# A two-layer encoder on one core: the products that add back to the residual stream, in seven products over pairs of pages

## The chip, the cores and the metric

The kernel runs on one core of one Trainium2 chip. The time is device microseconds (us) of one launch. Engines: PE (TensorE, matmuls), DVE (VectorE), ACT (ScalarE), POOL (GpSimd), SP (SyncE, which here only issues DMAs). Each engine works through its own queue in order; semaphores order the engines among each other. SBUF is the on-chip memory, PSUM the eight accumulator banks of PE, DRAM the memory behind the DMAs.

## The reference

1024 tokens, width 1024, two layers, all in float32:

```python
for layer in range(DEPTH):
    if layer % 2 == 0:                       # layer 0
        y = even_mixer(...)                  # attention (8 heads) and 2-D Fourier mixing, concatenated (1536 wide), @ w_out
    else:                                    # layer 1
        z = gelu(x @ w_in); u, v = split(z)  # 2048 wide each
        v = layer_norm(v); s = spatial mixing of v in chunks of 128 tokens + b_s
        y = (u * s) @ w_out                  # o_out in the kernel
    x = layer_norm(DN_ALPHA * x + y)
    x = layer_norm(DN_ALPHA * x + (silu(x @ w_gate) * (x @ w_up)) @ w_down)   # 2816 wide between
```

Four products go back to the 1024-wide stream: w_out (1536 to 1024), down of layer 0 (2816 to 1024), o_out (2048 to 1024), down of layer 1. They are what the change is about, and each ends with the residual and a layer norm.

## The kernel before

A product in float32 is made of three matmuls in a reduced format: each operand is split into a high part (a cast by ACT, L131) and a low part (the rest, a subtraction by DVE, L132), and `mm3` (L137 to L139) issues high x high, high x low, low x high. A matmul has a 128x128 stationary operand and up to 512 moving columns. Every operand that comes from DRAM or from another engine passes through such a split.

The hidden activations lie in DRAM as *pages*: a page is 128 hidden columns by all 1024 tokens, the hidden columns on the partitions. w_out reads 12 pages (`mix`), down 22 (`ha`, `hb`), o_out 16 (`tp`). A page's weight is 128 rows by 1024 columns.

`reduce` is the plain product over these pages. `load` brings in a pair of pages (two weights of 128x1024, and 512 tokens of both pages) and splits the three tiles; `mm` adds four tiles of 128 tokens by two halves of 512 columns to the eight PSUM banks, and this is done for each half of the tokens (`blk`). `residual` loads four tiles of the stream; POOL multiplies them by the gain of the last norm and adds its bias (L387, L388), for tokens 0 to 3 and 4 to 7 apart. `tail` adds the accumulators, makes the norm's statistics (L398, L399), normalises (L407) and stores the tile. `turn` calls `operands`: PE transposes the tile (L309), ACT scales it on the way out (L311), and DVE and ACT make the seven left operands of the next product from it.

What reads the stream (gate/up, u, v) goes *in seven products*, after Strassen and Winograd: a 2x2 block product made with seven block products in place of eight, and with sums of blocks. `operands` and `right_operands` make these sums, `seven` runs the products of one unit (A11, A12, S1, S2, A22, S4, S3 by `b11`, `b21`, `t1`, `t2`, `t4`, `b22`, `t3`), `kept` copies a bank to SBUF (L512), `emit` adds them up. Unit 0 of `ffn` runs in two halves of 256 columns, so that the first half of the tokens can start before the second is turned. `v_pair` does the same for v. In `spatial`, POOL multiplies u by the mixed v (L706) and stores the page (L709).

Order: instructions are issued in the order written and then moved by a scheduler that works with priorities, so each engine's queue is a mixture of neighbouring steps. PE runs w_out from 555 to 692 us, gate/up of layer 0 to 1126, down 0 to 1374, v to 1537, u and spatial mixing to 1728, o_out to 1935, gate/up of layer 1 to 2354, down 1 to 2600. Attention and Fourier mixing come before 555.

Of the kernel before, what the change touches and what calls it, by code (L numbers as in the profile page):

```python
# [9 lines left out]
F32 = mybir.dt.float32  # L10
# [102 lines left out]
class Trunk:  # L113
# [104 lines left out]
    def page_pair(self, p0, p1, blk):  # L218
        r = self.raw_tile()
        for i, p in enumerate((p0, p1)):  # L220
            self.nc.sync.dma_start(r[:, i * 512:(i + 1) * 512], p[:, blk * 512:(blk + 1) * 512])
        hi, lo = self.wpair()
        self.split(hi, lo, r)
        return hi, lo


    def run(self):
        tc, nc, a = self.tc, self.nc, self.a
        with ExitStack() as top:
# [14 lines left out]
            pages = [D_("ha", [P, S], 22), D_("tp", [P, S], 16), D_("hb", [P, S], 22)]  # L244
# [5 lines left out]
            with ExitStack() as ms:  # L250
# [5 lines left out]
                self.xo = tuple(xp.tile([P, 7, 2, 4, 256], F32R, name=f"xo{x}") for x in "hl")  # L256
                self.mp = ms.enter_context(self.pool("main", "right"))
                order = [8, 9, 10, 11, 0, 1, 2, 3, 4, 5, 6, 7]
                x_in = [a["x"][t * P:(t + 1) * P, :] for t in range(NT)]
                down = lambda l: [a["w_down"][l, j] for j in range(22)]  # L260
# [5 lines left out]
                pend = self.reduce([a["w_out"][k] for k in order], [mix[k] for k in order], x_in, None, (0, 0), xs[0], self.ahead, lambda: pre(0))  # L266
                self.ffn(w0[0], gate_up(0), pages[0], pend)
                vw = []
                pend = self.reduce(down(0), pages[0], xs[0], (0, 0), (0, 1), xs[1], None, lambda: vw.append(self.v_first()))
                left = self.spatial(vw[0], pages[1], pend)  # L270
                pend = self.reduce([a["o_out"][j] for j in range(16)], pages[1], xs[1], (0, 1), (1, 0), xs[2], None, lambda: pre(1), left)
                self.ffn(w0[1], gate_up(1), pages[2], pend)
                self.reduce(down(1), pages[2], xs[2], (1, 0), (1, 1), None)
# [8 lines left out]
    A11, A12, A22, S1, S2, S3, S4 = range(7)  # L282

# [3 lines left out]
    def turn_bank(self):  # L287

        i = (4, 5, 6, 7, 0, 1)[self.turns % 6]
        self.turns += 1  # L290
        self.stamp[i] = self.turns
        return self.bank(i)

    def m_tile(self, tag, bufs, shape):
        return self.mp.tile(list(shape), F32, tag=tag, name=self.name(tag), bufs=bufs)

    def x_tile(self):
        return self.m_tile("x", 4, (P, 1024))

    def operands(self, z, t, banks, gT, bT, A):  # L300

        nc = self.nc
        half, b, c = (t % 4) // 2, t // 4, slice(t % 2 * P, (t % 2 + 1) * P)
        xh, xl = self.xo
        op = lambda o: (xh[:, o, b, :, c], xl[:, o, b, :, c])
        w = self.m_tile("A", 2, (P, 8, P)) if half == 0 else self.x_tile().rearrange("p (k c) -> p k c", k=8)
        pss = [self.bank(i, (P, 4, P)) for i in banks]
        for k in range(8):
            nc.tensor.transpose(pss[k // 4][:, k % 4, :], z[:, k * P:(k + 1) * P], self.ident)  # L309
        for k in range(8):  # L310
            nc.scalar.activation(w[:, k, :], pss[k // 4][:, k % 4, :], AF.Identity, bias=bT[:, k:k + 1], scale=gT[:, k:k + 1])  # L311
# [8 lines left out]
        nc.vector.tensor_tensor(s, lo, hi, op=ALU.add)  # L320
        self.split(*op(self.S1), s)
        self.sub(s, s, a[:, 0:4, :])
        self.split(*op(self.S2), s)
        self.split(*op(self.A22), hi)
        self.sub(a[:, 4:8, :], a[:, 4:8, :], s)
        self.split(*op(self.S4), a[:, 4:8, :])
        self.sub(lo, a[:, 0:4, :], lo)
        self.split(*op(self.S3), lo)


    def reduce(self, ws, ps, resid, rgb, ln, keep, ahead=None, pre=None, left=()):

        left = list(left)
        nc, a = self.nc, self.a
        n = len(ws) // 2
        acc, A, xt, ops, z = {}, {}, {}, {}, {}
        xh, xl = self.xo
        flat = lambda o: tuple(x[:, o, 1].rearrange("p k c -> p (k c)") for x in (xh, xl))  # L340
        own = lambda: tuple(self.wx.tile([P, 1024], F32R, tag=t, name=self.name(t), bufs=1) for t in ("whi", "wlo"))
        sets = (lambda: [self.wpair() for _ in range(3)], lambda: [flat(o) for o in (2, 3, 4)], lambda: [flat(5), flat(6), own()])
        order = [0, 1, 2] * (n // 3) + [1, 2] if n % 3 == 2 else [0, 1, 2] * (n // 3 - 1) + [0, 1, 2]
        assert len(order) == n
        if keep is not None:
            gT, bT = (self.m_tile(x, 2, (P, 8)) for x in ("gT", "bT"))
            nc.gpsimd.dma_start(gT, a["ln_gT"][ln[0], ln[1]])
            nc.gpsimd.dma_start(bT, a["ln_bT"][ln[0], ln[1]])
        else:
            fg, fb = (self.bcast(self.m_tile("A", 2, (P, D)), a["ln_" + x][ln[0], ln[1]]) for x in "gb")  # L350
        self.less_weights()
        gb = self.pool("gb", "right")
        gp = gb.__enter__()
        if rgb is not None:
            rg, rb = (self.bcast(gp.tile([P, D], F32, name=self.name("r" + x)), a["ln_" + x][rgb[0], rgb[1]]) for x in "gb")

        def load(idx, blk):

            if (idx, blk) == (0, 0) and ahead is not None:
                ops[idx, blk] = ahead  # L360
                return
            pairs = sets[order[idx]]()
            u = []
            for i in range(2):
                r = self.raw(ws[2 * idx + i])
                self.split(*pairs[i], r)
                u.append(pairs[i])
            r = self.raw_tile()
            for i in range(2):
                self.nc.sync.dma_start(r[:, i * 512:(i + 1) * 512], ps[2 * idx + i][:, blk * 512:(blk + 1) * 512])  # L370
            self.split(*pairs[2], r)
            ops[idx, blk] = u, pairs[2]

        def mm(t, c, idx, i):
            us, (hh, hl) = ops[idx, t // 4]
            uh, ul = us[i]
            s, cc = slice(i * 512 + t % 4 * P, i * 512 + (t % 4 + 1) * P), slice(c * 512, (c + 1) * 512)
            if (t, c) not in acc:
                acc[t, c] = self.bank((0, 2, 4, 6, 2, 4, 6, 0)[t] + c)
            self.mm3(acc[t, c], (hh[:, s], hl[:, s]), (uh[:, cc], ul[:, cc]), idx == 0 and i == 0, idx == n - 1 and i == 1)  # L380

        def residual(ts):
            for t in ts:
                x = xt[t] = self.x_tile()
                nc.gpsimd.dma_start(x, resid[t])
# [4 lines left out]
        def tail(t, between=None):  # L390

            x, st = xt[t], self.small.tile([P, 2, 6], F32, tag="st", name=self.name("st"))
            for c in range(2):
                cc = slice(c * 512, (c + 1) * 512)
                for idx in (n - 2, n - 1):
                    for i in range(2):
                        mm(t, c, idx, i)
# [823 lines left out]
```

## Time and profile before

| | |
|---|---|
| median of 3 runs | 2611.92 us (2611.84 to 2617.37) |
| the profiled execution: its own time, its span | 2606.84 us, 2605.0 us |
| busy: PE, DVE, ACT, POOL | 2562.8, 1609.7, 1039.0, 362.4 us |
| granted PE clock, mean | 0.996 of full |
| moved by DMA | 293.5 MB, 113 GB/s on average |

The profile is one execution as the hardware profiler recorded it. A row of instructions has the line in the kernel, the engine, the operation, out<-in with the program's names (buffer numbers left out), the shape and count, then busy time in us and the mean of one in ns; behind the second bar stands how long the engine had idled ahead of these, and what ended it. A row of the timeline has the start in us, the time in us, and in brackets the idle time before. Matmuls are pipelined: one lasts longer than the distance to the next.

### The profile page before, as it was taken

How to read it: one execution, taken by the hardware profiler on the slowest of the kernel's cores; microseconds unless marked ns; L12 is line 12 of the kernel's file. 1: busy time of each engine (PE TensorE's matmuls, PEld its weight loads, DVE VectorE, ACT ScalarE, POOL GpSimd, SP SyncE). 2: the span in 40 equal slices, each digit the busy share in tenths (PEclk: the TensorE clock that was granted, in tenths of full speed). 3: DMA queues.
4: the chain of work that ended last, by engine and by line, in shares of the span. 5: the costliest groups of instructions: out<-in, count | busy, mean ns of one | idle time of the engine just before them, and what ended most of it. 6: DMA issues, size and time to landing. Idle time of an engine off the chain costs nothing.

```text
span 2605.0 us, 32916 instructions
## 1 busy us (share of the span) xinstructions
PE 2562.8 (98%) x12894; PEld 2156.7 (83%) x12894; DVE 1609.7 (62%) x2195; ACT 1039.0 (40%) x1609; POOL 362.4 (14%) x357
## 2 busy tenths in 40 slices
PE   9999999999999999999999999999999999999998
PEld 7878888888888888878789998878788888888877
DVE  4457677657765555564848667765785555546564
ACT  4335455545533333332526443333453333333221
POOL 1000000001000000030401025561400000003130
PEclk9999999999999999999999999999999999999999
DMA  5121111045222222255533244464532222235461
GB/s 174 39 84 44 33 39 43 21 148 187 96 93 86 73 89 75 93 192 167 182 125 122 85 128 140 138 207 160 175 117 89 81 82 81 81 119 186 148 213 70
DMA packets 98532, 293.51 MB, mean 113 GB/s; under 512 B 12712, under 2 KB 17480, under 8 KB 98376
## 3 DMA queue, kind: packets, MB, share of 16 engines
q1 hardware_dynamic: 75496, 213.23, 25.7%
q0 software_dynamic: 22880, 78.18, 8.1%
q8 instruction: 101, 1.65, 0.3%
q14 instruction: 55, 0.45, 0.1%
HBM read 223.72 MB, written 62.91 MB: 110 GB/s over the span
## 4 chain that ended last, share of the span: by engine, by line
PE 88%; DVE 5%; issue 3%; DMA 2%; POOL 1%; ACT 1%; SPq 0%; DVEq 0%; POOLq 0%; ACTq 0%
PE b L139 20%; PE b L137 20%; PE b L138 20%; PE b L751 6%; PE S L1137 6%; PE mm L137 4%; PE mm L138 4%; PE mm L139 4%; PE mm L1156 2%; DVE wlo L132 1%; DMA raw<-w_down 1%; DVE xol L132 1%; PE b L703 1%; PE b L309 1%; DVE st L399 0%
## 5 line engine op out<-in xcount | busy, mean ns | idle before, releaser
L139 PE MATMUL b<-xoh,wlo 128*128 128x512 f32 (+1 forms) x1928 | 746.5, 387 | 4.6 <-DVE wlo L132 4.6
L137 PE MATMUL b<-xoh,whi 128*128 128x512 f32 (+1 forms) x1928 | 747.7, 388 | 0.0
L138 PE MATMUL b<-xol,whi 128*128 128x512 f32 (+1 forms) x1928 | 745.2, 386 | 0.0
L132 DVE TENSOR_TENSOR wlo<-raw,whi 128x1024 fp32r<-128x1024 f32 (+2 forms) x353 | 445.9, 1268 | 462.0 <-ACT whi L131 437.0
L131 ACT CAST whi<-raw 128x1024 fp32r<-128x1024 f32 (+2 forms) x353 | 343.6, 976 | 716.9 <-PE b L138 480.1
L139 PEld LDWEIGHTS b<-xoh,wlo 128*128 128x128 f32 x1928 | 363.2, 188 | 83.2 <-DVE wlo L132 7.0
L137 PEld LDWEIGHTS b<-xoh,whi 128*128 128x128 f32 x1928 | 363.5, 189 | 76.6 <-DVE x L578 1.2
L138 PEld LDWEIGHTS b<-xol,whi 128*128 128x128 f32 x1928 | 363.2, 188 | 76.2 <-issue 0.2
L132 DVE TENSOR_TENSOR xol<-raw,xoh 128x1024 fp32r<-128x1024 f32 x130 | 167.1, 1305 | 174.5 <-ACT xoh L131 174.2
L131 ACT CAST xoh<-raw 128x1024 fp32r<-128x1024 f32 x130 | 133.6, 1053 | 258.8 <-PE b L139 123.1
L512 ACT COPY ct<-b 128x512 f32<-128x512 f32 (+1 forms) x240 | 136.9, 570 | 171.7 <-PE b L139 136.0
L139 PE MATMUL b<-xoh,xol 128*128 128x512 f32 x416 | 163.0, 392 | 3.3 <-DVE rs L201 3.3
L137 PE MATMUL b<-xoh 128*128 128x512 f32 x416 | 164.2, 395 | 0.0
L138 PE MATMUL b<-xol,xoh 128*128 128x512 f32 x416 | 162.4, 390 | 0.0
L127 DVE TENSOR_TENSOR raw<-raw,raw 128x512 f32<-128x512 f32 (+1 forms) x176 | 133.1, 756 | 24.8 <-DMA raw<-o_v 12.9
L137 PE MATMUL b<-whi,whi 128*128 128x512 f32 x320 | 127.3, 398 | 7.5 <-ACT whi L131 6.0
L139 PE MATMUL b<-whi,wlo 128*128 128x512 f32 x320 | 126.6, 396 | 4.0 <-DVE wlo L132 4.0
L751 PE MATMUL b<-whi,xoh 128*128 128x256 f32 x448 | 126.3, 282 | 0.0
L751 PE MATMUL b<-whi,xol 128*128 128x256 f32 x448 | 126.3, 282 | 0.0
L751 PE MATMUL b<-wlo,xoh 128*128 128x256 f32 x448 | 126.2, 282 | 0.0
L138 PE MATMUL b<-wlo,whi 128*128 128x512 f32 x320 | 126.1, 394 | 0.0
L573 DVE TENSOR_TENSOR ct<-b,ct 128x512 f32<-128x512 f32 (+1 forms) x92 | 61.3, 666 | 103.3 <-PE b L139 103.2
(278 smaller groups left out, 4023.3 us busy)
## 6 DMA issues: line engine op xcount, KB each, us to landing
raw<-w_down SPq DMA_DIRECT2D x88, 512.0 KB, 3.8
raw<-w_gate SPq DMA_DIRECT2D x44, 512.0 KB, 3.7
raw<-w_up SPq DMA_DIRECT2D x44, 512.0 KB, 3.6
raw<-o_out SPq DMA_DIRECT2D x32, 512.0 KB, 5.0
raw<-w_out SPq DMA_DIRECT2D x24, 512.0 KB, 5.7
xs<-x POOLq DMA_DIRECT2D x24, 512.0 KB, 2.9
x<-xs POOLq DMA_DIRECT2D x24, 512.0 KB, 4.6
ha<-x POOLq DMA_DIRECT2D x22, 512.0 KB, 2.9
```

Source lines behind the costliest of these rows:

```text
L127: self.nc.vector.tensor_tensor(out, a, b, op=ALU.subtract)
L131: self.nc.scalar.copy(hi, src)
L132: (eng or self.nc.vector).tensor_tensor(lo, src, hi.bitcast(F32), op=ALU.subtract)
L137: mm(ps, lh, rh, start=start, stop=False, skip_group_check=skip)
L138: mm(ps, lh, rl, start=False, stop=False, skip_group_check=skip)
L139: mm(ps, ll, rh, start=False, stop=stop, skip_group_check=skip)
L309: nc.tensor.transpose(pss[k // 4][:, k % 4, :], z[:, k * P:(k + 1) * P], self.ident)
L512: self.nc.scalar.copy(t, ps)
L573: nc.vector.tensor_tensor(sb, ps, sb, op=op)
L751: nc.tensor.matmul(ps[:, i * 256:(i + 1) * 256], l[:, o, b, k, c], r[:, k, :], start=start and k == 0 and i == 0 and m == 0, stop=k == 3 a ...
L1137: nc.tensor.matmul(sc[:, kb, :], l[:, s], r[:, kb * 512:(kb + 1) * 512], start=i == 0, stop=i == 4)
L1156: nc.tensor.transpose(ps[:, k, :], p[:, kt * P:(kt + 1) * P], self.ident)
```

## The change

All four `reduce` products now go in seven as well. Two pages form the 2x2 blocks with two halves of tokens: for pages h0, h1 (each cut into 512 tokens `lo` and 512 `hi`) and weights w0, w1 (each cut into two halves of the columns) there are seven products, each summed over all pairs of pages (in groups `g` of two pairs, the first of one if their number is odd) before the next one begins, in the order p = 1, 5, 6, 4, 7, 2, 3. A product has four slots of 128 tokens by 512 columns, so four PSUM banks. Sums of pages (SA, SB) and of weights (TA, TB) that the products need are made ahead by POOL (`combine`: two loads, four additions or subtractions of 128x512, two stores) and kept in DRAM; during attention for w_out, during gate/up for down, during v and u for o_out. The last pair's page sum is made while p = 1 runs.

```diff
+    def combine(self, tile, srcs, dsts, pages):
+        nc, lo, hi = self.nc, self.LO, self.HI
+        tt = nc.gpsimd.tensor_tensor
+        r0, r1 = tile(), tile()
+        for r, s in zip((r0, r1), srcs):
+            nc.gpsimd.dma_start(r, s)
+        if pages:
+            tt(r1[:, hi], r0[:, hi], r1[:, hi], op=ALU.add)
+            tt(r0[:, hi], r0[:, lo], r0[:, hi], op=ALU.subtract)
...
+        for r, d in zip((r0, r1), dsts):
+            nc.gpsimd.dma_start(d, r)
+    def source(self, st, p, m):
...
+        return {1: (h0[:, lo], w0[:, lo]), 2: (h1[:, lo], w1[:, lo]), 3: (sb[:, lo], w1[:, hi]), 4: (h1[:, hi], tb[:, lo]),
+                5: (sb[:, hi], ta[:, lo]), 6: (sa[:, lo], tb[:, hi]), 7: (sa[:, hi], ta[:, hi])}[p]
+    def stream(self, st, p, ms, raws, pairs):
...
+        for side in range(2):
+            r, (h, l) = raws(), pairs()
+            for i, m in enumerate(ms):
+                self.nc.sync.dma_start(r[:, i * 512:(i + 1) * 512], self.source(st, p, m)[side])
+            self.split(h[:, :n], l[:, :n], r[:, :n])
     def reduce(...):
-        sets = (lambda: [self.wpair() for _ in range(3)], lambda: [flat(o) for o in (2, 3, 4)], lambda: [flat(5), flat(6), own()])
...
+        for p in (1, 5, 6, 4, 7, 2):
+            for g in range(n):
+                load(p, g)
+                if p == 1 and g == 0:
...
+                    residual(0)
+                if p == 1 and g == 1:
+                    residual(1)
+                if p == 2:
+                    spread([lambda s=s: normed1(s) for s in slots], g, n)
+                for s in slots:
+                    mm(p, g, s)
...
+                if p == 1 and g == n - 1:
+                    self.page_job(st, M - 1)
+        for g in range(n):
+            load(3, g)
+            if g < n - 2:
+                for s in slots:
+                    mm(3, g, s)
+                spread([lambda s=s: turn1(s) for s in slots], g, n - 2)
...
+        return [lambda s=s: turn0(s) for s in slots], lambda: [sums(s) for s in slots]
     def ffn(...):
-            u0, u1 = unit(0, w0, 0), unit(0, w0, 1)
-            self.go(u0, 2)
-            pend[0]()
...
+        def store(j):
+            nc.gpsimd.dma_start(st["H"][j], page.pop(j))
+            if j % 2 == 0:
+                self.weight_job(st, j // 2, tile)
+            elif j >= 3:
+                self.page_job(st, j // 2 - 1, tile)
+        u0 = unit(0, w0, "yq")
+        turns[0]()
+        self.go(u0, 1)
+        turns[1]()
+        turns[2]()
+        self.go(u0, 1)
+        turns[3]()
```

Beside this, a unit of gate/up goes through its products in the order t4, t1, b11, b21, t2, b22, t3 with all 512 columns, unit 0 too; v goes in the order 4, 5, 1, 2, 6, 3, 7; the tiles of the second half of the tokens are turned during p = 3 (`turn1`), those of the first half (`turn0`) and the sums of both after it, inside the next stage. The tiles `x`, `y`, `q` take the place of `ct`, `A`, `S`.

What moves in the queues, at the two places that matter below. First POOL at the start of down 0; `x` are stream tiles, `xs` their copies in DRAM, `rg`, `rb` the gain and bias of the norm, `ha` the pages. Before:

```order
L583 DMA ha_134<-x_9304 128x1024
L385 DMA x_9585<-xs_3_92 128x1024
L387 TENSOR_TENSOR x_9573<-x_9573,rg_9418 128x1024
L387 TENSOR_TENSOR x_9577<-x_9577,rg_9418 128x1024
L388 TENSOR_TENSOR x_9573<-x_9573,rb_9420 128x1024
L388 TENSOR_TENSOR x_9577<-x_9577,rb_9420 128x1024
```

The same place after, from the store of the last page (`h_21`) on; `gb` are the gain and bias, `x_9712`, `x_9713` and `raw` the tiles of the sums:

```order
L636 DMA h_21_206<-x_9692 128x1024
L304 TENSOR_TENSOR x_9713<-x_9712,x_9713 128x512
L420 TENSOR_TENSOR x_9734<-x_9734,gb_9746 128x1024
L305 TENSOR_TENSOR x_9712<-x_9712 128x512
L421 TENSOR_TENSOR x_9734<-x_9734,gb_9748 128x1024
L306 TENSOR_TENSOR x_9712<-x_9713,x_9712 128x512
L420 TENSOR_TENSOR q_9736<-q_9736,gb_9746 128x1024
L307 TENSOR_TENSOR x_9713<-x_9713,x_9712 128x512
L314 DMA ffn0SA_216<-x_9712 128x1024
```

It ends, 14 multiplies and adds after the last page's store, with the sum of the last pair:

```order
L420 TENSOR_TENSOR x_9733<-x_9733,gb_9746 128x1024
L421 TENSOR_TENSOR x_9733<-x_9733,gb_9748 128x1024
L304 TENSOR_TENSOR raw_9965<-raw_9964,raw_9965 128x512
L305 TENSOR_TENSOR raw_9964<-raw_9964 128x512
L306 TENSOR_TENSOR raw_9965<-raw_9965,raw_9964 128x512
```

Before, four tiles went through POOL here and nothing of the product waited for them; now all eight do, and page sums stand between and behind them.

Second ACT where w_out ends and gate/up 0 begins; L311 (after: L337) is the scaling of a transposed tile, L131 the cast of an operand, L512 (L579) the copy of a bank. Before:

```order
L512 COPY ct_6488<-b_6475 128x256
L311 ACTIVATE x_6490<-b_6491,bT_5313,gT_5312 128x128 x4
L311 ACTIVATE x_6490<-b_6492,bT_5313,gT_5312 128x128
L131 CAST xoh<-S_6431 128x4x128
L311 ACTIVATE x_6490<-b_6492,bT_5313,gT_5312 128x128
```

After:

```order
L337 ACTIVATE x_6571<-b_6572,bT_5575,gT_5574 128x128 x4
L337 ACTIVATE x_6571<-b_6573,bT_5575,gT_5574 128x128 x4
L131 CAST xah_6569<-x_6571 128x4x128 x2
L337 ACTIVATE x_6609<-b_6610,bT_5575,gT_5574 128x128 x4
L337 ACTIVATE x_6609<-b_6611,bT_5575,gT_5574 128x128 x4
L131 CAST xah_6569<-x_6609 128x4x128 x2
L337 ACTIVATE q_6632<-b_6633,bT_5575,gT_5574 128x128 x4
L337 ACTIVATE q_6632<-b_6634,bT_5575,gT_5574 128x128 x2
L579 COPY y_6607<-b_6594 128x512
```

Before, one tile's scaling stands here among the copies of unit 0; after, the tiles of the first half are scaled here one behind the other, into `xah`, which the third product of unit 0 reads whole.

More of the change, by code (lines that the diff above doesn't have):

```diff
@@ L265, in pre @@
                     w0[l] = self.right_operands(*gate_up(l)(0))
[L266 to L271, printed above, removed]
@@ L272, in run, with pre_v @@
[L272 to L273 removed]
+                def pre_v():
+                    w0["v"] = self.v_begin(0)
+                G = self.stage
+                pend = self.reduce(G["mix"], x_in, None, (0, 0), xs[0], self.ahead, lambda: pre(0))
+                self.ffn(w0[0], gate_up(0), G["ffn0"], pend)
+                pend = self.reduce(G["ffn0"], xs[0], (0, 0), (0, 1), xs[1], None, pre_v)
@@ L302, in operands, with turned @@
+    def turned(self, z, banks, tile, gT, bT):
         nc = self.nc
[L303 to L306, printed above, removed]
+        w = tile.rearrange("p (k c) -> p k c", k=8)
         pss = [self.bank(i, (P, 4, P)) for i in banks]
@@ L323, in operands @@
[L323 to L331, printed above, removed]
-        left = list(left)
[L336 to L341, printed above, removed]
-        sets = (lambda: [self.wpair() for _ in range(3)], lambda: [flat(o) for o in (2, 3, 4)], lambda: [flat(5), flat(6), own()])
-        order = [0, 1, 2] * (n // 3) + [1, 2] if n % 3 == 2 else [0, 1, 2] * (n // 3 - 1) + [0, 1, 2]
-        assert len(order) == n
+        return w[:, 0:4, :], w[:, 4:8, :]
@@ new lines, in reduce, with pairs @@
+    def reduce(self, st, resid, rgb, ln, keep, ahead=None, pre=None, left=()):
+        nc, a = self.nc, self.a
+        lo, hi = self.LO, self.HI
+        left = list(left)
+        M = len(st["W"]) // 2
+        groups = [[0]] * (M % 2) + [[m, m + 1] for m in range(M % 2, M, 2)]
+        n = len(groups)
+        self.less_weights()
+        if self.xa is not None:
+            self.xpool.__exit__(None, None, None)
+        self.xpool = self.pool("rx", "left")
+        rx = self.xpool.__enter__()
+        cells = [tuple(x[:, b].rearrange("p k c -> p (k c)") for x in self.left(o)) for o in (4, 6, 5) for b in range(2)]
+        count = [0]
+        def pairs():
+            count[0] += 1
+            return cells[(count[0] - 1) % len(cells)]
+        raws = lambda: rx.tile([P, D], F32, tag="rx", name=self.name("rx"), bufs=6)
+        tmp = lambda: rx.tile([P, D], F32, tag="gb", name=self.name("gb"), bufs=2)
@@ L354, in reduce @@
[L354 to L360, printed above, removed]
-                return
[L362 to L385, printed above, removed]
+        token = lambda half, s: s // 2 * 4 + half * 2 + s % 2
@@ L386, in residual, with add @@
+        def add(half, s, c, p, first=False, op=ALU.add):
+            x = xt[half, s][:, c]
+            if first:
+                nc.vector.scalar_tensor_tensor(x, x, ALPHA, acc[p, s], ALU.mult, op)
+            else:
+                nc.vector.tensor_tensor(x, x, acc[p, s], op=op)
+        def residual(half):
+            for s in range(4):
+                x = xt[half, s]
+                nc.gpsimd.dma_start(x, resid[token(half, s)])
                 if rgb is not None:
@@ new lines, in ffn, with v_cells @@
+        turns[2]()
+        self.go(u0, 1)
+        turns[3]()
+        u1 = unit(1, self.right_operands(*weights(1)), "yq")
+        self.go(u1, 2)
+        sums()
+        self.go(u0, 5)
+        store(0)
+        self.go(u1, 5)
+        store(1)
+        for j in range(2, 22):
+            self.go(unit(j, self.right_operands(*weights(j))))
+            store(j)
+    def v_cells(self, pi):
+        a = self.a
+        b11, b12, b21, b22 = (self.raw(a["o_v"][pi * 4 + i]) for i in (0, 2, 1, 3))
+        w = {}
```

555 lines of the change are left out of this document (284 added, 271 removed).

## The prediction

> **What bounds the kernel now.** I read the page first (busy time by engine, then the chain that ended last), then busy time by stage.
>
> ```profile
> span 2605.0 us, 32916 instructions
> PE 2562.8 (98%) x12894; PEld 2156.7 (83%) x12894; DVE 1609.7 (62%) x2195; ACT 1039.0 (40%) x1609; POOL 362.4 (14%) x357
> PE 88%; DVE 5%; issue 3%; DMA 2%; POOL 1%; ACT 1%; SPq 0%; DVEq 0%; POOLq 0%; ACTq 0%
> ```
>
> TensorE is busy for 98% of the span and is 88% of the chain: matmuls taken off PE come off the time, unless PE then waits. The stages, cut where PE goes from one product to the next:
>
> ```profile
> 555.00:692.00 137.00, 137.00 (x633) 113.87 (x632) 90.25 (x120) 63.73 (x104) 15.35 (x26) 1.00 0.55 187
> 692.00:1126.00 434.00, 434.00 (x1964) 356.87 (x1964) 248.55 (x337) 174.53 (x259) 15.89 (x29) 1.00 0.27 91
> 1126.00:1374.00 248.00, 242.54 (x1083) 199.52 (x1082) 149.71 (x139) 86.35 (x124) 55.95 (x33) 0.99 0.47 156
> 1374.00:1537.00 163.00, 162.97 (x1366) 162.49 (x1365) 114.19 (x175) 80.46 (x125) 21.41 (x38) 1.00 0.34 115
> 1549.00:1728.00 179.00, 177.56 (x887) 148.66 (x885) 135.58 (x257) 66.31 (x95) 92.44 (x104) 1.00 0.47 149
> 1728.00:1935.00 207.00, 197.81 (x943) 164.44 (x942) 136.66 (x159) 84.12 (x141) 66.56 (x45) 0.98 0.48 159
> 1935.00:2354.00 419.00, 419.00 (x1841) 342.05 (x1840) 236.49 (x314) 160.99 (x228) 13.29 (x25) 1.00 0.29 95
> 2354.00:2600.00 246.00, 237.85 (x1037) 194.87 (x1035) 138.20 (x124) 57.66 (x57) 55.15 (x29) 0.99 0.45 151
> ```
>
> After the stretch come busy PE, weight loads, DVE, ACT, POOL, the granted clock, DMA share, GB/s. In order: w_out, gate/up 0, down 0, v, u with the spatial mixing, o_out, gate/up 1, down 1. The three reduces down 0, o_out and down 1 leave 5.46 + 9.19 + 8.15 = 22.8 us of PE idle; the rest nearly none. These three are also where POOL's multiplies and adds lie, and there DVE shows this (the first row is DVE's, the others POOL's):
>
> ```profile
> 1136.37 18.66 DVE L132 TENSOR_TENSOR wlo<-raw,whi 128x1024 fp32r<-128x1024 f32 x1 [5.29 <-ACT whi L131]
> 1135.02 4.80 POOL L387 TENSOR_TENSOR x<-x,rg 128x1024 f32<-128x1024 f32 x2
> ...
> 1149.19 4.75 POOL L388 TENSOR_TENSOR x<-x,rb 128x1024 f32<-128x1024 f32 x2
> ```
>
> Eight POOL operations of 4.76 / 2 = 2.38 us run back to back, and one DVE split is recorded for all of that time. The same place at other moments goes in turn:
>
> ```profile
> 1260.93 1.22 DVE L132 TENSOR_TENSOR wlo<-raw,whi 128x1024 fp32r<-128x1024 f32 x1
> 1262.06 2.90 DVE L320 TENSOR_TENSOR S<-x 128x512 f32<-128x512 f32 x1
> 1264.88 2.90 DVE L132 TENSOR_TENSOR xol<-x,xoh 128x512 fp32r<-128x512 f32 x1
> 1261.23 6.00 POOL L387 TENSOR_TENSOR x<-x,rg 128x1024 f32<-128x1024 f32 x2 [1.12 <-DMA x<-xs]
> ```
>
> The first split takes 1.22 us without POOL beside it; then each DVE operation waits out one POOL operation. So DVE with two inputs in SBUF and POOL tensor operations exclude each other: their times add.
>
> **The change, step by step.** Prices:
>
> ```profile
> 1084.70 0.39 PE L138 MATMUL b<-xol,whi 128*128 128x512 f32 x1
> ...
> 1088.19 0.39 PE L138 MATMUL b<-xol,whi 128*128 128x512 f32 x1
> L387 POOL TENSOR_TENSOR x<-x,rg 128x1024 f32<-128x1024 f32 x24 | 68.1, 2849 | 27.3 <-DMA x<-xs 27.3
> L706 POOL TENSOR_TENSOR x<-x,whi 128x512 f32<-128x512 f32 x16 | 22.4, 1399 | 24.4 <-DVE whi L704 16.2 <-PE b L138 7.4 <-issue 0.7
> L385 POOL DMA_DIRECT2D x<-xs x24 | 13.4, 558 | 46.2 <-issue 21.4 <-DMA xs<-x 10.7 <-DMA tp<-x 6.5
> L131 ACT CAST whi<-raw 128x1024 fp32r<-128x1024 f32 x291 | 304.9, 1051 | 597.5 <-PE b L138 385.6 <-PE mm L138 49.8 <-DMA raw<-w_down 46.2
> L132 DVE TENSOR_TENSOR wlo<-raw,whi 128x1024 fp32r<-128x1024 f32 x291 | 402.7, 1389 | 288.8 <-ACT whi L131 263.9 <-POOL x L706 12.0 <-PE mm L1156 6.2
> L127 DVE TENSOR_TENSOR raw<-raw,raw 128x512 f32<-128x512 f32 x156 | 108.9, 698 | 11.7 <-DMA raw<-o_u 6.5 <-DMA raw<-w_up 2.0 <-DVE wlo L704 0.8
> L694 DVE TENSOR_SCALAR wlo<-wlo,vmv,vrs 128x128 f32<-128x128 f32 x64 | 26.3, 492 | 3.9 <-DMA wlo<-vd 3.9
> L131 ACT CAST xoh<-A 128x512 fp32r<-128x512 f32 x36 | 21.6, 651 | 2.4 <-DVE A L127 2.4
> L311 ACT ACTIVATE x<-b,bT,gT 128x128 f32<-128x128 f32 x96 | 36.2, 478 | 5.4 <-PE b L309 5.4
> ha<-x POOLq DMA_DIRECT2D x22, 512.0 KB, 2.9
> raw<-ha SPq DMA_DIRECT2D x44, 256.0 KB, 3.9
> tp<-x POOLq DMA_DIRECT2D x16, 512.0 KB, 3.5
> raw<-tp SPq DMA_DIRECT2D x32, 256.0 KB, 4.3
> ```
>
> Fewer matmuls. Before, the reduces take 72 pages x 48 = 3456 matmuls of 512 columns; after, 36 pairs x 7 products x 4 slots x 3 = 3024. The two rows are the first and the last of 16 starts in a stretch without a wait: (1088.19 - 1084.70) / 15 = 0.233 us for a matmul. 432 x 0.233 = **-100 us**: 16.8 in w_out (6 pairs), 30.7 in each down (11 pairs), 22.3 in o_out (8). Unit 0 of the gate/up stages, now done whole, keeps its columns: 0.
>
> The waits that the three reduces have now lose their place: between 0 and -22.8; the last one's end stays, so **-20**.
>
> What is added on other engines: 72 sums on POOL, each 2 loads, 4 operations of 512 columns, 2 stores, all in POOL's one queue. On DVE the additions of product banks to the tiles grow in number; they read PSUM on one side, and they come at the ends of products, beside 12 matmuls each: 0 but for what is named below. On SP the loads become more and smaller (256 KB for 512), 0.52 MB per pair and product of 12 x 0.233 = 2.79 us, which is 188 GB/s; the w_out row shows 187 with PE never idle: 0.
>
> Start of down 0 and down 1. All eight residual tiles now go through POOL when the reduce starts, mixed with the last page sums, and every sum must be stored before the second product (p=5) ends. After the last page's store stand 14 residual operations, 8 of a sum and 8 DMA issues: 14 x 2.38 + 8 x 1.3 + 8 x 0.55 = 48 us; the last page is ready some 4 us after the reduce starts and landings on the way hold the queue some 5 (estimates, from the landing rows), the store 2.9, the load 3.9, cast and split 1.05 + 1.22: 66. PE needs it when p=1 and all but the last group of p=5 (9 of 11 pairs) are done: 30.7 + 9 x 2.79 = 56. So 10 us even if DVE costs POOL nothing. DVE has about 20 splits of 1.22 us in that time; one for one they add 24, but some come before the tile loads land: ends 10 and 31 a stage, taken **24 each, 48**. What is queued behind POOL there: nothing PE needs before.
>
> By the Trainium skill (SBUF — State Buffer, Who interferes with whom), the engine that issues first keeps the shared ports for its whole instruction, and the other fully blocks. The trace agrees at 1262 (2.9 us against 2.4 of POOL's one operation), not at 1136, where eight went by. With the page's rule alone a split waits for one POOL operation at most and each such stage would lose about 24; with starvation up to 31, by the rows above.
>
> Start of o_out: the last four spatial multiplies stand behind 14 residual operations: 14 x 2.38 + 9 x 1.3 + 7 us of issues and landings = 52 until the last page is stored, then its landing 3.5, the load for the sum 4, the sum 5.2, its landing 3.5, load and split 4.3 + 2.3: 75. PE gets to it after p=1 (22.3), three of the four groups of p=5 (16.8) and two groups of p=6, which stand ahead (11.2): 50. Ends 20 and 36 (with the splits), taken **30**.
>
> The two gate/up starts. Before, half of the tokens are turned before the reduce ends; now all four turns of the first half, for ACT 4 x (8 x 0.478 + 2 x 0.651) = 20.5 us, come after its last product, and A11 reads all four. PE has 24 matmuls (5.6 us) and 32 transposes of 128 columns (at least a quarter of a 512-column matmul, 1.9; taken as 3) to cover them: about 12 us of waiting. After such a wait PE runs slower for a while:
>
> ```profile
> 1282.42 0.50 PE L137 MATMUL b<-whi,whi 128*128 128x512 f32 x1 [2.71 <-ACT whi L131]
> ...
> 1284.70 0.63 PE L137 MATMUL b<-whi,whi 128*128 128x512 f32 x1
> ...
> 1287.69 0.53 PE L138 MATMUL b<-wlo,whi 128*128 128x512 f32 x1
> ```
>
> (Seven steps in 2.99 us, 0.43 each: about +2 with the first ones.) Ends 10 and 22, taken **15 each, 30**. The same at v, where A11 comes third, with weight sums on POOL beside it: ends 5 and 20, **13**. In w_out, the shortest reduce, POOL's last sums and the normalisation's DVE work lie in p=2 and p=3: ends 0 and 10, **5**.
>
> u with the mixing: per group PE has 177.56 / 8 = 22 us; POOL now has 8 operations x 1.3 = 10.4. DVE has 4 subtractions (L127, 2.8), splits of 3.5 tiles (4.3) and 16 normalisations of v (L694, 64 for each of two tiles over 8 groups, 0.49: 7.9): 15. Together 25, 3 over what PE has, 24 in 8 groups; but part of DVE's work reads PSUM or meets POOL waiting for a DMA. Ends 0 and 36 (store-to-load waits on POOL added), half of 24 taken: **12**. Sums beside gate/up and attention: in the 434 us of a gate/up stage, 39 for two units, DVE has 248.55 / 11 = 23 and POOL gets 8 x 1.3 = 10.4: 33 together fit, but not always at the right moment: ends 0 and 20, **6**.
>
> Sum: -100 - 20 + 48 + 30 + 30 + 13 + 5 + 12 + 6 = +24. The profiled execution took 2606.8 us (span 2605.0), so 2631; the median of the runs is 5 above it, so **2636**. All lower ends give -55, 2557; all upper ends +108, 2720.
>
> **Rivals.** (a) Faster: POOL's chain is not late, because the residual tiles' loads and the splits leave gaps that the sums fill, and waits come to half: -120 + 72 = -48, 2564. For it: waits of before hid mostly; the split of 18.66 us cost PE little:
>
> ```profile
> 1156.21 0.50 PE L139 MATMUL b<-whi,wlo 128*128 128x512 f32 x1 [1.61 <-DVE wlo L132]
> ```
>
> Against: there POOL had nothing that PE needed, now it has. It holds if the last page sum is stored within about 50 us of the start of a down stage.
> (b) Much slower: starvation as at 1136 in every start and the u stage bound by POOL: upper ends of these, 14 + 6 + 14 and 24 over the sum, 2694.
> (c) The stalls just cancel the gain: 24 less of them, 2612.
>
> **How the numbers follow.** My sum 0.42, (a) 0.36, (b) 0.14, (c) 0.08. The sum and (b) are slower, (a) faster, (c) neither. A measurement of this kernel tells about 0.2% (5 us) from no change. Faster 0.36, same 0.08, slower 0.56. The likeliest one's own range is 2617 to 2660; the range over the cases, with (a) and most of (b), is 2558 to 2685.
>
> **What would show it.** PE with 432 fewer 512-column matmuls, and busy time some 100 us less; DVE splits of over 5 us beside POOL multiplies at the start of each reduce; PE idle of 20 us or more ahead of the p=5 or p=6 products of the three later reduces, released by a split of a page sum; about 13 us ahead of the third product of each gate/up stage, released by ACT; gaps of 1 to 4 us in u. If PE is idle for less than 90 us over the reduces' starts and the gate/up starts together, rival (a) holds and my forecast is wrong. If the gap at a down start is under 10 us, the price of the shared ports was too high; if PE is busy by less than 80 us below before's, the price of a matmul was.

## The result, and the profile after

The changed kernel takes 2724.89 us (median of four runs, 2715.09 to 2726.9) against 2611.88: the ratio is 1.042, 95% interval 1.0392 to 1.0453, 4% slower. The prediction had 2636 us, in a range from 2558 to 2685, and 2720 with every upper end: the side was right, the size was not. Of the runs below, one of the nine executions of "all on DVE, sums of u as changed" took 8659.72 us, as no other did, and the ratios leave it out.

The head of the page after, and its granted clock:

```profile
span 2723.9 us, 33140 instructions
PE 2520.8 (93%) x12294; PEld 2103.8 (77%) x12294; DVE 1803.6 (66%) x2305; ACT 1068.3 (39%) x1643; POOL 950.6 (35%) x932
PEclk9989999999999999988999998988899999999899
```

PE has 600 instructions fewer, as it should (432 of 512 columns in the reduces; 336 of 256 turned into 168 of 512 in unit 0). At 0.233 us each the reduces' 432 are 100 us. But PE's busy time fell by only 42.0 us, and its idle time rose from 2605.0 - 2562.8 = 42.2 to 2723.9 - 2520.8 = 203.1. So the span grew by 161 of idle less 42 = 119. Most of the 58 us between 100 and 42 are matmuls that ran slowly. In the two traces, 181 matmuls of 512 columns before and 361 after start more than 0.3 us ahead of the next one without a wait between them; over 0.233 us each they cost 26 us before and 67 after, so 40 of the 58 are found there. The rest was not told apart. The stages (stretch; busy PE, PEld, DVE, ACT, POOL; clock; DMA share; GB/s), from the front to down 1, without gate/up 1:

```profile
0.00:583.40 583.40, 554.20 (x3106) 474.17 (x3107) 357.29 (x558) 256.65 (x471) 111.83 (x114) 0.97 0.28 93
583.40:718.30 134.90, 122.46 (x539) 99.77 (x539) 98.39 (x128) 59.96 (x85) 22.83 (x29) 0.96 0.65 229
718.30:1159.40 441.10, 433.77 (x1882) 352.98 (x1881) 291.01 (x340) 176.05 (x270) 176.06 (x192) 0.99 0.50 181
1159.40:1412.50 253.10, 223.93 (x957) 182.19 (x956) 175.05 (x176) 98.50 (x128) 73.43 (x49) 0.94 0.60 205
1412.50:1584.80 172.30, 166.21 (x1377) 165.47 (x1376) 125.58 (x176) 83.85 (x141) 91.00 (x108) 0.98 0.58 203
1584.80:1808.00 223.20, 196.81 (x902) 160.75 (x901) 147.92 (x260) 65.02 (x95) 138.67 (x144) 0.92 0.47 155
1808.00:2025.90 217.90, 170.99 (x739) 138.74 (x738) 140.60 (x161) 73.99 (x101) 85.07 (x62) 0.89 0.60 208
2469.40:2723.90 254.50, 218.12 (x925) 177.31 (x923) 172.44 (x172) 77.70 (x83) 75.06 (x46) 0.93 0.58 201
```

Where PE is idle most (down 0, u, o_out, down 1), the mean clock is lowest. The longest gap and what follows it, in o_out:

```profile
1916.57 0.79 PE L137 MATMUL b<-xoh 128*128 128x512 f32 x1 [20.31 <-ACT xoh L131]
1917.16 0.63 PE L138 MATMUL b<-xol,xoh 128*128 128x512 f32 x1
1917.59 0.63 PE L137 MATMUL b<-xoh 128*128 128x512 f32 x1
```

After the wait matmuls start 0.43 us apart, not 0.233. The granted clock is 0.50 from 1916.6 to 1921.0 us and 1.00 from there to 1930; in the wait itself it is 0.61 on average.

What that gap waits for. POOL's rows, then SP's, then ACT's:

```profile
1886.88 0.59 POOL L762 DMA_DIRECT2D tp<-x  x1
...
1907.75 0.55 POOL L314 DMA_DIRECT2D oddSB<-raw  x1
1911.60 0.32 SPq L355 DMA_DIRECT2D rx<-oddSB  x1
1913.18 1.05 ACT L131 CAST xoh<-rx 128x1024 fp32r<-128x1024 f32 x1 [23.98 <-DMA rx<-oddSA]
...
1915.47 2.98 ACT L131 CAST xoh<-rx 128x1024 fp32r<-128x1024 f32 x3 [0.29 <-DMA rx<-oddSB]
```

It is the late page sum. The store of the last page (`tp`) is issued 79 us after the reduce began at 1808.2, that of its sum 100 us after, and PE goes on at 108, when the sum is loaded and cast.

Why DVE is late at the start of down 0. First DVE's rows, then POOL's beside the second of them:

```profile
1165.64 3.48 DVE L132 TENSOR_TENSOR xol<-rx,xoh 128x1024 fp32r<-128x1024 f32 x3
1173.19 18.99 DVE L132 TENSOR_TENSOR xol<-rx,xoh 128x1024 fp32r<-128x1024 f32 x8 [1.84 <-ACT xoh L131]
1204.37 0.69 DVE L411 SCALAR_TENSOR_TENSOR y<-y,b 128x512 f32<-128x512 f32 x1 [9.25 <-POOL y L421]
...
1207.66 13.29 DVE L132 TENSOR_TENSOR xol<-rx,xoh 128x1024 fp32r<-128x1024 f32 x4
...
1170.50 3.11 POOL L420 TENSOR_TENSOR x<-x,gb 128x1024 f32<-128x1024 f32 x1 [0.24 <-DMA x<-xs]
1173.58 2.28 POOL L305 TENSOR_TENSOR x<-x 128x512 f32<-128x512 f32 x1
1175.81 3.38 POOL L421 TENSOR_TENSOR x<-x,gb 128x1024 f32<-128x1024 f32 x1
```

The last four splits take 13.29 us, 3.3 each, where one alone takes 1.22; POOL's operations are stretched too (3.38 for 2.39, 2.28 for 1.28): the two go in turn. Ahead of these splits DVE stands still for 9.25 us: the addition of the first product to the residual tile `y` (L411) comes before them in its queue, and POOL finishes that tile only then. What PE makes of it, with the release of the last sum:

```profile
1214.35 0.79 PE L138 MATMUL b<-xol,xoh 128*128 128x512 f32 x1 [9.08 <-DVE xol L132]
1232.11 0.79 PE L138 MATMUL b<-xol,xoh 128*128 128x512 f32 x1 [4.28 <-DVE xol L132]
1244.51 0.80 PE L137 MATMUL b<-xoh 128*128 128x512 f32 x1 [5.55 <-ACT xoh L131]
...
1235.08 0.54 POOL L314 DMA_DIRECT2D ffn0SB<-raw  x1
1238.90 0.32 SPq L355 DMA_DIRECT2D rx<-ffn0SB  x1
```

The first wait ends with the second of the four splits. Stretching explains 5.8 us of it at most (a weight split of 2.77 us and two of 3.32, for three of 1.22); the stand at `y` delayed all of them. In the second, too, PE waits for stretched splits; ACT's cast ahead of them had waited for a weight sum for v, which DVE took 3.42 us over. The third is for the sum of the last pair, whose load could be issued only at 1238.9, 79.5 us after the reduce began; a weight for v, cast by ACT ahead of it, waited for a tile that the same store held (SP waits 16.1 us for it). Down 1 has the same pair: 7.55 us after a stand of 9.23 us at `y`, and 11.86 us for the last sum.

### The profile page after: what moved, and what is told of

Same layout as the page of the kernel before. It is cut to its first block, busy times and chain, and to the rows that moved or that the text cites. A ratio compares the mean times of both kernels' runs of the same rounds, so it can differ in the third digit from the quotient of the medians.

```text
span 2723.9 us, 33140 instructions
## 1 busy us (share of the span) xinstructions
PE 2520.8 (93%) x12294; PEld 2103.8 (77%) x12294; DVE 1803.6 (66%) x2305; ACT 1068.3 (39%) x1643; POOL 950.6 (35%) x932
## 5 line engine op out<-in xcount | busy, mean ns | idle before, releaser
L132 DVE TENSOR_TENSOR xol<-rx,xoh 128x1024 fp32r<-128x1024 f32 (+1 forms) x264 | 367.5, 1424 | 185.2 <-ACT xoh L131 182.4
L132 DVE TENSOR_TENSOR wlo<-raw,whi 128x1024 fp32r<-128x1024 f32 (+3 forms) x265 | 328.6, 1244 | 207.0 <-ACT whi L131 202.4
L137 PE MATMUL b<-xoh 128*128 128x512 f32 x1000 | 398.3, 402 | 62.7 <-ACT xoh L131 62.0
L138 PE MATMUL b<-xol,xoh 128*128 128x512 f32 x1000 | 402.0, 402 | 49.8 <-DVE xol L132 49.8
L131 ACT CAST whi<-raw 128x1024 fp32r<-128x1024 f32 (+3 forms) x265 | 249.7, 953 | 493.1 <-PE b L138 198.3
L131 ACT CAST xoh<-rx 128x1024 fp32r<-128x1024 f32 (+1 forms) x264 | 254.4, 1005 | 463.2 <-PE b L138 303.6
L137 PE MATMUL b<-xoh,whi 128*128 128x512 f32 x1040 | 415.4, 399 | 12.6 <-ACT whi L131 11.3
L138 PE MATMUL b<-xol,whi 128*128 128x512 f32 x1040 | 412.2, 396 | 0.0
L139 PE MATMUL b<-xoh,wlo 128*128 128x512 f32 x1040 | 411.1, 396 | 1.2 <-DVE wlo L132 1.1
L139 PE MATMUL b<-xoh,xol 128*128 128x512 f32 x1000 | 398.3, 399 | 0.5 <-DVE xol L132 0.5
L579 ACT COPY y<-b 128x512 f32<-128x512 f32 x200 | 115.3, 585 | 180.6 <-PE b L139 175.7
```

Of the source, the lines that this page charges most:

```text
L131: self.nc.scalar.copy(hi, src)
L132: (eng or self.nc.vector).tensor_tensor(lo, src, hi.bitcast(F32), op=ALU.subtract)
L137: mm(ps, lh, rh, start=start, stop=False, skip_group_check=skip)
L138: mm(ps, lh, rl, start=False, stop=False, skip_group_check=skip)
L139: mm(ps, ll, rh, start=False, stop=stop, skip_group_check=skip)
L579: nc.scalar.copy(t, ps)
```

## The experiments

For reading them, the length of each stage in us, cut at the same events in every trace: the first matmul of each reduce, and the last transpose of the tiles turned behind it (in "kernel before" that is behind the last tile of the second half); down 1 ends with the last matmul. Times are of the launch, beside a run of the kernel before on the same chip. All but the first two and the last two rows are single executions; the kernel before differs by 8.5 us from chip to chip, and the changed kernel's four executions by 12, so differences of less than about 10 us in the whole time are not read.

| run | time (before) | front | w_out | gate/up 0 | down 0 | v and u | o_out | gate/up 1 | down 1 |
|---|---|---|---|---|---|---|---|---|---|
| kernel before | 2611.9 | 555.0 | 145.0 | 421.2 | 265.0 | 333.1 | 208.6 | 421.2 | 246.1 |
| changed kernel | 2724.9 (2611.9) | 583.5 | 143.8 | 432.1 | 265.1 | 383.7 | 227.8 | 433.4 | 243.2 |
| neither sums nor residual | 2542.0 (2609.2) | 562.2 | 140.5 | 432.0 | 227.2 | 339.1 | 179.3 | 431.8 | 214.8 |
| no sums | 2592.0 (2609.2) | 557.7 | 139.3 | 431.3 | 248.7 | 339.9 | 199.6 | 432.2 | 228.9 |
| no additions of sums | 2644.1 (2609.2) | 573.2 | 140.8 | 432.0 | 248.5 | 347.9 | 227.7 | 431.8 | 229.2 |
| no residual arithmetic | 2643.5 (2609.2) | 581.4 | 145.9 | 437.0 | 226.5 | 385.7 | 202.0 | 438.0 | 213.9 |
| residual on DVE | 2685.0 (2603.4) | 579.3 | 145.0 | 436.9 | 243.9 | 383.4 | 213.8 | 438.1 | 231.3 |
| residual and sums on DVE | 2652.5 (2603.4) | 566.5 | 146.4 | 433.0 | 249.3 | 365.6 | 207.6 | 435.6 | 235.4 |
| p=4 second | 2696.4 (2603.4) | 577.3 | 140.9 | 432.0 | 262.0 | 382.9 | 220.3 | 434.0 | 233.8 |
| both of these | 2639.3 (2603.4) | 565.5 | 141.5 | 433.2 | 249.4 | 363.4 | 206.1 | 433.1 | 233.9 |
| earlier page sums in u, rope on DVE | 2724.1 (2603.4) | 570.7 | 146.9 | 432.6 | 267.3 | 389.2 | 226.9 | 433.2 | 244.1 |
| p=4 second, residual spread, POOL | 2698.6 (2603.4) | 585.4 | 138.1 | 432.4 | 257.9 | 384.3 | 213.2 | 434.1 | 240.0 |
| all moves, all on DVE | 2598.9 (2603.4) | 570.5 | 141.3 | 435.7 | 228.5 | 368.5 | 192.8 | 434.8 | 213.8 |
| the same, sums on POOL | 2643.1 (2603.4) | 571.8 | 137.8 | 435.6 | 236.2 | 387.6 | 202.2 | 437.2 | 221.2 |
| all on DVE, sums of u as changed | 2601.6 (2607.9) | 568.9 | 141.6 | 435.8 | 229.4 | 369.4 | 194.6 | 435.2 | 213.6 |
| all on DVE, sums of u in place | 2568.8 (2607.9) | 565.4 | 140.8 | 436.0 | 229.3 | 341.2 | 192.3 | 433.0 | 215.0 |

**Taking away.** Four kernels, each derived from the changed one.

```diff
 def source(...):                                  # neither, no sums
-        sa, sb, ta, tb = (st[n][m] for n in ("SA", "SB", "TA", "TB"))
+        sa, sb, ta, tb = h0, h1, w0, w1           # and combine() returns at once
 def residual(half):                               # neither, no residual arithmetic
-                    nc.gpsimd.tensor_tensor(x, x, rg, op=ALU.mult)
-                    nc.gpsimd.tensor_tensor(x, x, rb, op=ALU.add)
 def combine(...):                                 # no additions
-        tt = nc.gpsimd.tensor_tensor
+        tt = lambda *a, **k: None
```

> Leaves out all page and weight sums (the seven products read the pages and weights themselves) and POOL's multiply and add of the residual tiles; the products, their loads and splits, and their order stay. Theory A (POOL's arithmetic shuts DVE out of SBUF, so splits come late) and theory B (POOL's queue of loads and stores and the tiles that it shares make others wait) both expect PE idle to fall from 203 us to below 80 and the time to about 2545. Theory C (the seven products themselves are at fault: their loads, or the turning left for the next stage) expects over 2620, with PE idle still above 120.

Measured: 2541.99 us. Theory C falls. The head of its page:

```profile
span 2540.1 us, 32330 instructions
PE 2472.5 (97%) x12294; PEld 2076.6 (82%) x12294; DVE 1613.0 (64%) x2305; ACT 1074.3 (42%) x1643; POOL 245.9 (10%) x308
```

The same 12294 PE instructions now take 2472.5 us, 90 less than before, with 2540.1 - 2472.5 = 68 of idle. So the products pay for themselves by 67 us on the same chip, and the 183 us by which the changed kernel is slower than this one lie in the sums and the residual's arithmetic. Gate/up stays 10 to 17 us longer than before in every variant: the turning left for its start is most of it (with neither, too, PE waits 7.33 us there for ACT, and runs slowly behind that). w_out has a wait of 8.26 us for the load of its second group of pages, 8.25 with neither: that is the products' own.

> Leaves out all page and weight sums, with their loads and stores; POOL's residual arithmetic stays. A: 288 operations of 1.3 us go, but the 48 of 2.4 us at the starts stay and block DVE: about 2620. B: nearly all of the loss goes, about 2570.

> Leaves out only the additions of the sums; their loads and stores on POOL's queue and their tiles stay. A: close to the run without sums, within 15 us of it. B: close to the changed kernel, above 2690.

> Leaves out POOL's multiply and add of the residual tiles (38 us of POOL at each of three starts); loads stay, sums stay. A: the starts of down 0, o_out and down 1 lose half of their PE idle, together about 60 us with the slow clock behind it: about 2660. B: within 15 us of the changed kernel, since the late sums of the last pages hang on DMAs.

Measured: 2592.0, 2644.1, 2643.5 us. Neither theory has it alone. The sums cost 2724.9 - 2592.0 = 133 us: 81 for their additions, 52 for their loads, stores and tiles. The residual's arithmetic costs 81 beside the sums but 50 without them. In the downs nothing of the loss is left without it: they take 226.5 and 213.9, like the run with neither. It does not make all of it alone: without the sums it costs them 21.5 and 14.1 us, with the sums 38.6 and 29.3. In v and u the residual costs nothing and the sums everything (339.9 without, 347.9 without their additions). Theory B's "within 15 us" for the run without residual is refuted; so is A's "within 15 us" for the run without additions.

**Moving to DVE, and the order.** 

```diff
-                    nc.gpsimd.tensor_tensor(x, x, rg, op=ALU.mult)     # and the add: residual on DVE
+                    nc.vector.tensor_tensor(x, x, rg, op=ALU.mult)
-        tt = nc.gpsimd.tensor_tensor                                   # sums on DVE
+        tt = nc.vector.tensor_tensor
-        for p in (1, 5, 6, 4, 7, 2):                                   # p=4 second
+        for p in (1, 4, 5, 6, 7, 2):
```

> The residual's multiply and add go from POOL to DVE, nothing is left out. A: 16 operations of about 1.2 us of DVE for 16 of 2.4 of POOL that block DVE: near the run without them (2643), at most 20 above. If DVE's own time is what is short, not the exclusion, the 48 x 1.2 = 58 us come back and the time is above 2690.

> The residual's arithmetic and the additions of the sums all go to DVE; POOL keeps the DMA issues. A: only the part of the queue and the shared tiles stays, 2542 + 52 = 2594, and DVE's own 258 us of additional work hides: 2590 to 2620. B: DVE now waits in its queue for the sums' loads, in front of the splits: above 2660.

> The changed kernel with the products in the order 1, 4, 5, 6, 7, 2, 3: the first product that needs a page sum comes third in place of second, 30.7 us later. The late sum of the last pages (PE gaps of 9.4, 20.7 and 12.3 us, with the slow clock behind them some 48) is in time: about 2680. If the splits that POOL blocks are what is late there, the wait only moves: above 2710.

> Both: arithmetic on DVE, and p=4 ahead of p=5. A: some 15 to 30 us under the run with the arithmetic on DVE alone, 2570 to 2600, and so faster than the kernel before.

Measured: 2685.0, 2652.5, 2696.4, 2639.3. With both moved, DVE gets 257 us of work more (48 x 1.21 and 288 x 0.69, what one operation takes on DVE undisturbed), and the kernel gets 72 us faster, 64 if each is compared with the kernel before on its own chip. The head of its page:

```profile
PE 2502.5 (94%) x12294; PEld 2091.6 (79%) x12294; DVE 1836.7 (69%) x2641; ACT 1077.1 (41%) x1643; POOL 398.8 (15%) x596
```

DVE is busy only 33 us longer than in the changed kernel, because that one's DVE is stretched: its 2305 instructions take 1803.6 us there and 1613.0 with neither. So time on DVE is not what is short. How much of the gain is the end of the exclusion, and how much comes from sums and residual tiles being ready sooner (each operation takes about half as long on DVE), these runs do not tell apart. The expectations of A were too good: by 16 to 39 us beyond their slow ends.

Giving the page sums 30.7 us more alone brings 20 to 28 us. In down 1 the wait of 11.86 us is gone. In o_out another of 17.56 us takes the place of the one of 20.31: product 4 reads the last pages themselves, and these too are stored late, behind the residual's operations in POOL's queue. PE's row, then ACT's:

```profile
1880.65 0.80 PE L137 MATMUL b<-xoh 128*128 128x512 f32 x1 [17.56 <-ACT xoh L131]
1879.55 2.94 ACT L131 CAST xoh<-rx 128x1024 fp32r<-128x1024 f32 x3 [13.02 <-DMA rx<-tp]
```

**Queue and tiles.** 

```diff
 spatial():                                        # earlier page sums in u
+                    if g > 1 and i == 0:
+                        self.page_job(st, g - 2)
...
-                if g > 1:
-                    self.page_job(st, g - 2)
 rotate_b():                                       # rope on DVE
-        nc.gpsimd.tensor_tensor(w, w, s, op=ALU.mult)
+        nc.vector.tensor_tensor(w, w, s, op=ALU.mult)
 reduce():                                         # residual spread, one tile at a time
+                if p == 1: spread([lambda s=s: residual(1, s) for s in slots], g, n)
+                if p == 4: spread([lambda s=s: residual(0, s) for s in slots], g, n)
...                                                # and add(0, s, lo, 1, True) moved from the end of p=1 to the end of p=5
```

> The changed kernel with two steps moved: in the u stage a pair's page sum is issued at the start of a group, not at its end, so that its two tiles are stored before the next group's weights want a tile of the same ring of four; and the ten rope multiplies of attention go from POOL to DVE, so that they don't stand in POOL's queue behind loads of the sums. B (shared tiles and queue): u and mixing lose 10 to 20 of their 40 us of PE gaps, attention 10 to 15 of its 28 us: about 2695. A (ports alone): no more than 5 in each: above 2713.

Measured: 2724.1. The front falls by 12.8 us, u and mixing grow by 5.5, and small shifts elsewhere eat the rest. For the front the trace of the changed kernel shows why; POOL's rows, then DVE's and PE's:

```profile
188.05 0.53 POOL L302 DMA_DIRECT2D raw<-w_out  x1 [3.53 <-DMA mixSB<-raw]
188.60 1.27 POOL L993 TENSOR_TENSOR rw<-rw,rope_s 128x512 f32<-128x512 f32 x1
189.91 0.69 DVE L994 TENSOR_TENSOR rt<-rt,rw 128x512 f32<-128x512 f32 x1 [6.97 <-POOL rw L993]
193.77 0.58 PE L137 MATMUL mm<-whi,ckv0h 128*128 128x256 f32 x1 [5.61 <-ACT rt L984]
```

The rope multiply stood in POOL's queue behind a load that itself waited for a tile, and DVE waited 7 us for it. In u my reading (the sum issued too late) was not borne out.

> Order 1, 4, 5, 6, 7, 2, 3, and the residual tiles one by one over p=1 (second half of tokens) and p=4 (first half), the first product's addition moved behind p=5; all arithmetic stays on POOL. If it is the bunching of the residual operations at the start that starves the splits, down 0, o_out and down 1 fall by 15 to 25 each against the run with the order alone: about 2640. If each POOL operation costs DVE its time wherever it stands, within 15 of that run (2696).

> Order and spreading as in the run before this one, the earlier page sums in u, and the additions, the residual and the rope multiplies on DVE. If the parts add, 2639 less 45 for the three starts, 15 for u and 5 for attention: about 2575, faster than the kernel before. If what is left of the loss is DVE's own time and the loads of the sums, above 2620.

> As the run before this one, but the additions of the sums stay on POOL; only the residual and the rope multiplies are on DVE. It parts the cost of the sums' place from that of the residual's: A expects 20 to 40 above the run before this one, most of it in u; if the sums on POOL are harmless once the residual is gone and their tiles come free in time, the same within 10.

Measured: 2698.6, 2598.9, 2643.1. On POOL, spreading the residual brings nothing. Its trace, DVE, POOL and PE in down 0:

```profile
1207.68 0.69 DVE L411 SCALAR_TENSOR_TENSOR q<-q,b 128x512 f32<-128x512 f32 x1 [17.94 <-POOL q L420]
...
1213.49 8.01 DVE L127 TENSOR_TENSOR raw<-raw,raw 128x1024 f32<-128x1024 f32 x1
...
1213.47 2.35 POOL L419 TENSOR_TENSOR x<-x,gb 128x1024 f32<-128x1024 f32 x1
1215.78 2.34 POOL L420 TENSOR_TENSOR q<-q,gb 128x1024 f32<-128x1024 f32 x1
1218.07 2.33 POOL L420 TENSOR_TENSOR x<-x,gb 128x1024 f32<-128x1024 f32 x1
1223.82 0.80 PE L138 MATMUL b<-xol,xoh 128*128 128x512 f32 x1 [21.20 <-DVE xol L132]
```

DVE first stands still for 17.94 us, at an addition to a residual tile that POOL has not finished. Then a subtraction of 1.22 us (a weight sum for v, ahead of the splits in DVE's queue) waits through three POOL operations in a row; PE's 21 us end with a split behind both. In this run DVE waits 49 us in all for residual tiles of POOL, in the changed kernel 23: spreading brought the tiles later as well as farther apart, so it does not decide the question that it was to test. With the arithmetic on DVE the same spreading takes the downs to 228.5 and 213.8, the lengths of the run with neither. With the sums back on POOL 44 us return, 19 of them in v and u. The expectation of 2575 was missed by 24 us: u.

The last two test what u loses.

```diff
 mixed():                                          # sums of u in place
-                    nc.gpsimd.dma_start(st["H"][j], pg.pop(j))
+                    nc.gpsimd.dma_start(st["H"][j], pg[j])
+                    if j % 2 == 1:
+                        r0, r1 = pg.pop(j - 1), pg.pop(j)
+                        self.sums_of(nc.vector.tensor_tensor, r0, r1, True)   # the four additions of combine
+                        nc.gpsimd.dma_start(st["SA"][j // 2], r0)
+                        nc.gpsimd.dma_start(st["SB"][j // 2], r1)
...                                                # and the page_job calls of this stage are left out
```

> As the run with order, spreading and all arithmetic of sums, residual and rope on DVE, but with the page sums of u issued at a group's end, as in the changed kernel. The two runs that differ in this place (2719 and 2723 of span) say that the earlier issue costs u about 5 us: about 2594. If it was chance, 2599.

> As the run before, but the page sums of u and mixing are made in place, in the tiles of the two pages as they leave the mixing, after the pages' own stores: no loads back from DRAM and no tile of the weights' ring. If the round trip through DRAM and the shared ring of four raw tiles is what u loses (theory B, in the form that the moved issue did not reach), v and u fall from 368 to about 350 us and the start of o_out a little too: about 2575. If it is DVE's time and order (A), v and u stay above 360: 2590 or more.

Measured: 2601.64 and 2568.76 us, ratios to the kernel before 0.9962 (0.9948 to 0.9976) and 0.9852 (0.9834 to 0.9869). Where in a group the page sums of u are issued makes no difference (v and u take 369.4 us, and 368.5 with the earlier issue): that was chance. In the last run, the same additions by the same engine, but without the loads back and without the ring of four weight tiles: v and u fall from 369.4 to 341.2 us, down to the 339.1 of the run with neither. So with the arithmetic on DVE the round trip through DRAM and its tiles is what is left of the loss in u; the additions' place in DVE's queue moved with them, which was not tried by itself. In the changed kernel it looks like this, DVE, then PE:

```profile
1653.44 0.69 DVE L127 TENSOR_TENSOR raw<-raw,raw 128x512 f32<-128x512 f32 x1 [5.67 <-DMA oddSA<-raw]
1657.44 0.79 PE L137 MATMUL b<-xoh,whi 128*128 128x512 f32 x1 [5.92 <-ACT whi L131]
```

DVE, in order, holds at a weight sum whose tile is still being stored by POOL's queue. Of PE's 26 us of idle in u, 11.3 stand behind weights that are late like this one. A longer one lies beside o_out's 20 us:

```profile
1910.22 0.69 DVE L127 TENSOR_TENSOR raw<-raw,raw 128x512 f32<-128x512 f32 x1 [22.20 <-DMA oddSA<-raw]
```

That is a sum for the next gate/up weights, already in DVE's queue, and nothing of DVE runs for 22 us. But it is not what PE waits for there. PE's gap ends with ACT's cast of the page sum, whose load waited for the same store (SP stands 21.2 us for it). And with p=4 second DVE holds at such a sum for only 7.6 us, while PE still waits 17.56.

The version with the sums in place beats both kernels: 1.5% under the one before.

## Why the prediction was right in sign and wrong in size

The step that failed is the price of the stalls: +144 us in the sum, 228 with all upper ends. Stage by stage, what the sum gives against what the table shows (matmuls saved and the slow clock included): front at most +6 and +28.5; w_out -12 and -1.2; the gate/up stages +15 each and +10.9, +12.2; down 0 -12 and +0.1; v and u +25 and +50.6; o_out -1.5 and +19.2; down 1 -12 and -2.9. The side was right because the stalls that it named outweigh the matmuls, but most were named for a shorter delay or with another cause.

**Fewer matmuls, -100.** Right in number, and 0.233 us holds where PE doesn't wait. But busy PE fell 58 us less, some 40 of it by the slow matmuls behind waits. I had seen them (0.43 us apart for eight matmuls) and counted them at the two gate/up starts only, as +2 each. There are 34 waits of over 1 us. The check that I gave (busy PE down by less than 80 means a wrong price for a matmul) was wrong for the same reason.

**Down 0 and down 1, 24 each.** Priced too low: 37.9 and 28.4 us against the run with neither. The delay of the last sum was right: its store is issued 75 us after the start, and my sum gives 57, or 81 with 24 for the splits; splits of 3.3 us, one POOL operation each, were in it too. The sign that I gave, splits of over 5 us, did not come: no split of the changed kernel lasts over 3.6. What the sum lacked is DVE's stand of 9.25 and 9.23 us at the residual tile `y`, with the splits behind it, and the clock. By the runs this loss needs the residual's arithmetic, and the sums' additions beside it nearly double it.

**o_out, 30.** Mechanism right, mis-sized: 48.5 us against the run with neither, and PE idle rose from 9.2 to 46.9. I had the last page stored 52 us after the start and its sum split at 75; the store was issued at 79 and PE went on at 108.

**u with the mixing, 12, and v, 13.** The step that failed most: 50.6 us together. For u I had added up port times (25 us against 22 of PE in a group) and taken half of the excess; v had the turning and the weight sums. The runs put 36 us on the additions and 8 on loads and stores when taken one by one, and 28 on the round trip once the additions are on DVE. DVE held at a weight sum, because a store still reads its tile, had no place in my sum. What the rest of the 36 is made of stays open.

**Front, part of 6.** Measured 28.5. I had looked for room on POOL and DVE, which there is (before, in the order of the stage rows: DVE 351 and POOL 22 of 555 us):

```profile
0.00:555.00 555.00, 542.04 (x3106) 464.70 (x3107) 350.91 (x559) 258.62 (x472) 22.11 (x24) 1.00 0.19 58
```

The rope multiplies wait for loads in POOL's queue: it isn't a busy engine but a blocked one. Moving them brought 12.8 us; without any additions the front still takes 18.2 us longer than before, without the sums altogether 2.7, so more than half of the loss goes with the sums' loads and stores.

**Gate/up starts, 15 each.** Right within about 4: 10.9 and 12.2, with this wait for ACT in gate/up 0 and one of 6.97 us in gate/up 1:

```profile
734.85 0.80 PE L137 MATMUL b<-xah,whi 128*128 128x512 f32 x1 [7.33 <-ACT xah L131]
```

**w_out, 5, and before's own waits, -20.** w_out has 12.4 us of PE idle instead of 5, 8.26 of them the load of its second group of pages; larger waits took the place of those of before.

**The rivals.** (b), starvation in every start and POOL as the bound of u, was nearest in time at 2694 and right that u would be hit harder, but not by its mechanism: no split starved in the changed kernel, and POOL is busy for 138.67 of the 223.20 us of u. (a) needed the last page sum stored within about 50 us of a down's start; it took 79.5. The rule of the Trainium skill that I weighed (SBUF — State Buffer, Who interferes with whom: the later of two fully blocks for the whole instruction of the first) agrees with the splits at 3.3 us; the wait of 8.01 us over three POOL operations, in the run with the residual spread, again goes beyond it, as at 1136 in the kernel before.

## What to carry to other kernels

Moving side work to an idle engine isn't free if that engine shares a memory path, an in-order queue or a ring of tiles with the work that feeds the bottleneck. Here POOL's work beside DVE stretched DVE's own by 190 us of busy time, and doing the same arithmetic on the busier DVE was cheaper. Price a stall with the slow clock behind it. Before putting jobs with loads into an in-order queue, look for whatever short operation stands behind them, and in the other engines' queues for operations that wait for these jobs with urgent ones behind. What is already in SBUF should be summed there: the in-place sums of u brought v and u down by 28 us.

## What the runs showed of the hardware

DVE, one operation of 1.22 us, can stay shut out by a row of POOL operations (8.01 us beside three, 18.66 beside eight), although the two take turns in other stretches, in all splits of the changed kernel among them; what decides between the two wasn't found. The same 128x1024 multiply took 1.21 us on DVE and 2.39 on POOL.
